# First mixer of a hybrid decoder step: the samples' split operand moved to its source, the states scaled on VectorE, a third of the weights' low parts built by adding loads

## The chip, the cores and the metric

The kernel runs on one core of a Trainium2 chip. The metric is the device time of one execution in microseconds. The engines are named as in the profile: PE (TensorE, matmuls; PEld is its weight load), DVE (VectorE), ACT (ScalarE), POOL (GpSimd), SP (SyncE, which only issues DMAs here).

## The reference, cut to what matters

The program is one inference step of a two-layer decoder on 512 prompt tokens and 8 sequences of 4 sample tokens (T = 544 columns). Each layer is a token mixer and a squared-ReLU MLP. Layer 0 has a Mamba-2 mixer, layer 1 an HGRN2 mixer. The change is in the Mamba-2 mixer:

```python
proj = u @ w_in                                   # 1024 x 5152: gates z, x, B, C, dt
xbc  = silu(conv4(x | B | C) + conv_b)
# chunked scan, for 32 heads in 4 groups
w = (C B^T) * exp(cum_i - cum_j) * dt             # inside a chunk
y = w @ x + (C h) * exp(cum)                      # from the state before it
h = exp(cum_last) * h + sum_j tail_j x_j B_j^T    # state after it
y = group_rmsnorm((y + D * x) * silu(z)) @ w_out
```

The states of the 8 sample sequences go through the same recurrence: `h = decay * h + outer(tail * x, B)`.

## The kernel before

**Products.** All columns sit in tiles of 128 x 544. A weight unit is a tile of 128 x 1024 (512 KB) that SP loads to `raw`. It is split in two parts that TensorE can multiply at one pass each: ACT casts `whi`, and `wlo = raw - whi` is taken by DVE, or, for the units 6, 9, ... 54 of the first mixer (`3 < u < U_MLP`, `u % 3 == 0`, 17 of its 56 units), by POOL. `products` then does hi x hi, hi x lo and lo x hi for each of 8 (or 2 x 4) row tiles and two column halves: 48 matmuls of 128 x 272 a unit.

**Order.** `ORDER` lists the mixer's units by hand: 4 gate units z, 6 input units i (four of x, then B and C) and 4 output units o for each of 4 groups. `conv_unit` splits the weights one to two units ahead of the product, and issues the loads from a list (`loads`), by a number ahead. Beside the products run generators: `scan(g)` (the recurrence of group g) and `gated_norm(g)`. `products` calls `tick()` after every 12 matmuls, which steps them; `yield pace` in them says after how many ticks the next piece follows. From that program a scheduler with priorities orders each engine's instructions; engines run their lists strictly in order, and semaphores carry the dependences.

**The scan of a group.** `tokens(c)` transposes x of chunk c (`pxt`) and scales it to `xd` (DVE) and `xt` (ACT, 8 small operations). `weights(c)` loads `w` (cumulated decays, 8 heads x 128 x 128) and makes relu and exp of it on ACT; `weighted(c)` multiplies by `cb` on DVE. `inside(c)` adds to the state `hT` (`pu`; its scaling by `dec` on POOL) and to the outputs (`py`). `before(c)` loads the decays a second time as `E`, takes exp, and adds the old state's part (`pi`).

For the samples `xts` is made from `pxs`, and later, two pieces on, `xq`, its hi and lo parts in 32-row bands (ACT cast, then two DVE subtractions of 32 x 512 on the other bands). `psi` reads the old states `st` (four tiles of two sequences). Then POOL scales all four `st` by the decays, and in four steps two matmuls `pn` (`bm` x `xq`, PSUM tiles from the pool `mx` of 4, which `pu`, `py`, `psi`, `pi` share) are added by DVE to `st`, which SP stores.

Of the kernel before, what the change touches and what calls it, by code (L numbers as in the profile page):

```python
# [16 lines left out]
P = 128  # L17
D = 1024
# [78 lines left out]
def trunk(ctx: ExitStack, tc: tile.TileContext, io):  # L97
# [65 lines left out]
    mp = {}  # L163

# [25 lines left out]
    def conv_unit():  # L190
        if state["conv"] >= len(jobs):
            return
        (kind, u), at = jobs[state["conv"]]
        state["conv"] += 1
        with tc.high_priority() if u > 2 else ExitStack():
            while state["load"] <= min(at + (3 if mp else 1), len(loads) - 1):
                if loads[state["load"]][0] != "u" and not mp:
                    break
                load_next()
        with tc.high_priority() if u > 2 and not mp else ExitStack():  # L200
            if kind == "u":
                raw = loaded.pop(("u", u))
                hi = wcv.tile([P, 1024], F32R, tag="whi", name=f"whi{u}")
                lo = wcv.tile([P, 1024], F32R, tag="wlo", name=f"wlo{u}")
                for a in (0, 512) if u < 2 else (None,):
                    c = slice(None) if a is None else slice(a, a + 512)
                    split(raw[:, c], hi[:, c], lo[:, c], nc.gpsimd if 3 < u < U_MLP and u % 3 == 0 else None)
            else:
                hi, lo = form(kind, u)
        ready[kind, u] = (hi, lo)  # L210

# [66 lines left out]
    def products(ps, hi, lo, ops, first, last):  # L278

        n = len(ops)  # L280
        for k, (oh, ol) in enumerate(ops):
            for j, (w, o) in enumerate(((hi, oh), (hi, ol), (lo, oh))):
                for h in range(2):
                    nc.tensor.matmul(  # L284
                        ps[:, h, :HF], w[:, k, :], o[:, h * HF : (h + 1) * HF],
                        start=(first and k == 0 and j == 0), stop=(last and k == n - 1 and j == 2),
                    )
            if k % 2:
                tick()
# [49 lines left out]
    def add_squares(t, first, name):  # L339
        if first:  # L340
            nc.scalar.activation(ssq[:, :T], t, AF.Square)
        else:
            sq = nt.tile([P, 568], F32, tag="t", name=name)[:, :T]
            nc.scalar.activation(sq, t, AF.Square)
            nc.vector.tensor_tensor(ssq[:, :T], ssq[:, :T], sq, ADD)
# [32 lines left out]
    def ssd(then):  # L378
# [5 lines left out]
        wdt = pool.tile([P, KT, NS], F32, tag="cm", name="wdt")  # L384
# [5 lines left out]
        seqcol = cp.tile([P, SEQS, NS], F32, name="seqcol")  # L390
        nc.sync.dma_start(seqcol, io["seqcol"])
# [37 lines left out]
        def conv_tile(u, ct, dst, rep):  # L429

            hi, lo = unit(u)
            ps = acc_tile(f"ps{u}")
            products(
                ps, hi.rearrange("p (k m) -> p k m", m=P), lo.rearrange("p (k m) -> p k m", m=P), uops, True, True
            )
            pre = p2.tile([P, 571], F32, tag="pre", name=f"pre{ct}")
            sv = pre[:, 515:571].rearrange("p (s t) -> p s t", t=7)
            nc.gpsimd.memset(pre[:, 0:3], 0.0)
            nc.scalar.copy(pre[:, 3:275], ps[:, 0, :HF])
            nc.scalar.copy(pre[:, 275:515], ps[:, 1, :240])  # L440
# [3 lines left out]
            acc = pool.tile([P, 568], F32, tag="cacc", name=f"cacc{ct}")  # L444
            wc = V_CONVW - V_CONVB + ct
            nc.scalar.activation(acc, pre[:, 0:568], AF.Identity, bias=vh[:, ct : ct + 1], scale=vh[:, wc : wc + 1])
            for i in range(1, 4):
                nc.vector.scalar_tensor_tensor(acc, pre[:, i : i + 568], vh[:, wc + 24 * i : wc + 24 * i + 1], acc, MUL, ADD)
            th = nt.tile([P, 568], F32, tag="t", name=f"th{ct}")
# [3 lines left out]
            for s0, n in ((0, 7), (7, 1)):  # L453
                a = [t[:, 515 + 7 * s0 : 515 + 7 * s0 + (7 * n if n > 1 else 4)] for t in (th, acc)]
                if n > 1:
                    a = [t.rearrange("p (s t) -> p s t", t=7)[:, :, 0:4] for t in a]
                    d = dst[:, NP_ : NP_ + 28].rearrange("p (s t) -> p s t", t=4)
                else:
                    d = dst[:, NP_ + 28 : T]
                nc.vector.scalar_tensor_tensor(d, a[0], 1.0, a[1], ADD, MUL)  # L460
# [18 lines left out]
        def silu2(u, zs, z):  # L479

            th = nt.tile([P, 568], F32, tag="t", name=f"thz{u}")[:, :T]
# [3 lines left out]
        def first_gates():  # L485
# [11 lines left out]
            background(rstd_steps(1.0 / D, "sn", res, cp, wait=2), "sn", wait=2)  # L497
# [15 lines left out]
        def normed():  # L513

            for k in range(KT):
                t = pool.tile([P, T], F32, tag="st", bufs=4, name=f"xn{k}")
                if k % 3 == 1:
                    nc.gpsimd.tensor_tensor(t, x[k], rb, MUL)
                    scaled_split(t, vec[:, V_NMIX0 + k : V_NMIX0 + k + 1], *new_uops(k, "s"))
                else:  # L520
                    nc.vector.scalar_tensor_tensor(t, x[k], vec[:, V_NMIX0 + k : V_NMIX0 + k + 1], rb, MUL, MUL)
                    split(t, *new_uops(k, "s"))
                yield 0.8
# [3 lines left out]
        def scan(g, BT, CT, xs, par):  # L527
# [5 lines left out]
            sts, ws_, xds, xts = [], [], [], []  # L533
            hT = pool.tile([P, 512], F32, tag="hT", name=f"hT{g}")

            def weights(c):

                w = pool.tile([P, 8, P], F32, tag="w", bufs=2, name=f"w{g}_{c}")
                nc.sync.dma_start(w, cum_d[hs, c * P : (c + 1) * P].partition_broadcast(P))
# [3 lines left out]
                ws_.append(w)  # L543

            def tokens(c):
# [9 lines left out]
                for h in range(8):  # L555
                    nc.scalar.activation(xt[:, h], pxt[:, h * 64 : (h + 1) * 64], AF.Copy, scale=ttok[:, c, 8 * g + h : 8 * g + h + 1])
# [3 lines left out]
            def inside(c):  # L560
# [18 lines left out]
            def before(c):  # L579

                cs = slice(c * P, (c + 1) * P)
                E = pool.tile([P, 4, P], F32, tag="E", bufs=2, name=f"E{g}_{c}")
                src = cum_d[hs, cs].rearrange("(j o) t -> o j t", o=2)
                for o in range(2):
                    nc.sync.dma_start(E[64 * o : 64 * o + 64], src[o].partition_broadcast(64))
                nc.scalar.activation(E, E, AF.Exp)
# [12 lines left out]

            tokens(0)  # L600
            weights(0)
            yield pace
# [14 lines left out]
            nc.scalar.copy(bt.rearrange("p a b -> p (a b)"), pbt)  # L617
            cb = pool.tile([P, 4, P], F32, tag="cb", name=f"cb{g}")
# [6 lines left out]
            inside(0)  # L625
            yield pace
# [4 lines left out]
            weights(2)  # L631
            yield pace
            inside(1)
            yield pace
# [4 lines left out]
            weights(3)  # L639
            yield pace  # L640
            inside(2)
            yield pace
# [3 lines left out]
            cm = pool.tile([P, SEQS, NS], F32, tag="cm", name=f"cm{g}")  # L646
            nc.vector.tensor_tensor(cm, CT[:, sc].unsqueeze(1).to_broadcast([P, SEQS, NS]), seqcol, MUL)
# [10 lines left out]
            )  # L658
            pbs = mx(f"pbs{g}")
# [7 lines left out]
            ws = pool.tile([NS, 8, NS], F32, tag="ws", name=f"ws{g}")  # L667
# [13 lines left out]
            xq = pool.tile([P, 8, 64], F32R, tag="xt", bufs=2, name=f"xq{g}")  # L681
            nc.scalar.copy(xq, xt)
            for r in (32, 96):
                rs = slice(r, r + 32)
                nc.vector.tensor_tensor(xq[rs], xt[rs], xq[rs].bitcast(F32), SUB)
            yield pace
            psi = mx(f"psi{g}")
            for s in range(SEQS):
                c = s % 4
                nc.tensor.matmul(  # L690
                    psi[32 * c : 32 * c + 32, :], cm[:, s], sts[s // 2][:, s % 2], start=(s < 4), stop=(s >= 4),
# [5 lines left out]
            )  # L697
            for q in range(4):
                nc.gpsimd.tensor_tensor(
# [3 lines left out]
            yield 2 * pace  # L703
            for q in range(4):
# [173 lines left out]
        for u, (kind, g, j) in enumerate(ORDER):  # L878
# [3 lines left out]
            else:  # L882
                {"i": input_unit, "z": gate_unit, "o": out_unit}[kind](u, g, j)
        es.close()
# [633 lines left out]
```

## Time and profile before

| | |
|---|---|
| runs | 1583.47, 1586.29, 1589.55 us (median 1586.29) |
| profiled execution | 1590.45 us, of which the span of instructions is 1588.7 us |
| PE busy | 1547.5 us, 97% |
| DVE / ACT / POOL busy | 1099.3 / 741.9 / 187.9 us |
| TensorE clock granted | 0.985 on average |

Times within the trace count from the span's start. The first mixer fills about the first 500 us; then follow MLP, second mixer, MLP. "Idle ... <-" names the work that ended last before an instruction could start. A window's row gives for each engine the busy time and, in brackets, the number of instructions; PEclk is the granted clock of TensorE as a share of the full one.

### The profile page before, as it was taken

The page shows a single profiled execution, that of the slowest core. Times are in us where ns is not written, and L with a number is a line of the kernel's source. Part 1 is how long each engine was busy: PE and PEld are TensorE (multiplying, and loading weights), DVE is VectorE, ACT ScalarE, POOL GpSimd, SP SyncE. Part 2 cuts the span into 40 slices and gives each one's busy share as a digit, 9 for nine tenths or more (in the row PEclk, how much of TensorE's full clock was granted, in tenths as well). Part 3 has the DMA queues.
Part 4 walks back from the last instruction along what each step waited for, and adds up shares of the span by engine and source line. Part 5 has one row for each costly group of instructions (what it writes and reads, how often), then busy time and mean ns, then how long its engine had stood idle before and what let it go on. Part 6 is the DMA issues. An engine that isn't in the chain of part 4 may idle for free.

```text
span 1588.7 us, 32391 instructions
## 1 busy us (share of the span) xinstructions
PE 1547.5 (97%) x13420; PEld 1482.7 (93%) x13420; DVE 1099.3 (69%) x1962; ACT 741.9 (47%) x1431; POOL 187.9 (12%) x208
## 2 busy tenths in 40 slices
PE   8898989999999999999999999999999999999997
PEld 7896879999999999999999999999999999999997
DVE  7888787877887747464565688888878655474644
ACT  5585663757434526353463333333335436273552
POOL 4323141232311001010000000000001001010001
PEclk9998998999999999999999999999999999999998
DMA  5353435354236236344323232323226335453311
GB/s 185 104 164 105 159 88 187 102 176 143 74 120 175 91 107 172 94 136 104 112 64 126 67 96 83 98 83 116 77 94 173 88 106 153 120 160 80 120 54 57
DMA packets 88116, 183.28 MB, mean 115 GB/s; under 512 B 12641, under 2 KB 39297, under 8 KB 87969
## 3 DMA queue, kind: packets, MB, share of 16 engines
q1 hardware_dynamic: 79792, 167.49, 33.7%
q0 software_dynamic: 6912, 12.59, 4.9%
q8 instruction: 105, 1.72, 0.5%
q10 hardware_dynamic: 1264, 1.14, 0.2%
q14 instruction: 43, 0.34, 0.1%
HBM read 164.00 MB, written 17.18 MB: 114 GB/s over the span
## 4 chain that ended last, share of the span: by engine, by line
PE 71%; DVE 4%; ACT 1%; DMA 1%; issue 1%; POOL 0%; POOLq 0%; SPq 0%; ACTq 0%; DVEq 0%
PE pd L284 22%; PE ps L284 15%; PE pp L973 11%; PE pm L284 6%; PE pc L973 4%; PE pho L284 3%; PE po L284 2%; PE pa L1112 1%; DVE wlo L188 1%; ACT whi L187 1%; DMA raw<-in_W 1%; PE pS L1215 0%; PE po L1238 0%; PE pa L1131 0%; PE pd L1342 0%
## 5 line engine op out<-in xcount | busy, mean ns | idle before, releaser
L187 ACT CAST whi<-raw 128x1024 fp32r<-128x1024 f32 (+1 forms) x178 | 185.0, 1039 | 344.7 <-PE ps L284 110.7
L188 DVE TENSOR_TENSOR wlo<-raw,whi 128x1024 fp32r<-128x1024 f32 (+1 forms) x161 | 200.5, 1245 | 31.0 <-ACT whi L187 27.0
L284 PE MATMUL pd<-gh,wlo 128*128 128x272 f32 x992 | 205.5, 288 | 0.9 <-DVE wlo L188 0.6
L284 PE MATMUL pd<-gh,whi 128*128 128x272 f32 x992 | 205.7, 287 | 0.0
L284 PE MATMUL pd<-gl,whi 128*128 128x272 f32 x992 | 205.0, 288 | 0.0
L284 PEld LDWEIGHTS pd<-gh,wlo 128*128 128x128 f32 x992 | 155.7, 188 | 2.2 <-DVE wlo L188 2.2
L284 PEld LDWEIGHTS pd<-gh,whi 128*128 128x128 f32 x992 | 156.2, 188 | 0.0
L284 PEld LDWEIGHTS pd<-gl,whi 128*128 128x128 f32 x992 | 155.6, 188 | 0.0
L284 PE MATMUL ps<-uh_s,whi 128*128 128x272 f32 x576 | 127.4, 303 | 1.6 <-DVE zs L503 0.8
L373 DVE TENSOR_TENSOR x<-pd,x 128x544 f32<-128x544 f32 x62 | 44.7, 722 | 121.3 <-PE pd L284 121.3
L284 PE MATMUL ps<-ul_s,whi 128*128 128x272 f32 x576 | 122.5, 294 | 0.5 <-DVE ul_s L188 0.5
L284 PE MATMUL ps<-uh_s,wlo 128*128 128x272 f32 x576 | 121.7, 293 | 0.0
L180 POOL DMA_DIRECT2D v<-in_W x48 | 42.3, 1045 | 593.0 <-DMA v<-in_W 448.6
L284 PE MATMUL ps<-uh,whi 128*128 128x272 f32 x512 | 112.2, 300 | 0.0
L284 PE MATMUL ps<-uh,wlo 128*128 128x272 f32 x512 | 106.8, 288 | 0.0
L284 PE MATMUL ps<-ul,whi 128*128 128x272 f32 x512 | 106.4, 289 | 0.0
L284 PEld LDWEIGHTS ps<-uh_s,whi 128*128 128x128 f32 x576 | 93.0, 194 | 9.7 <-issue 5.6
L284 PEld LDWEIGHTS ps<-ul_s,whi 128*128 128x128 f32 x576 | 93.6, 195 | 1.0 <-DVE ul_s L188 0.7
L284 PEld LDWEIGHTS ps<-uh_s,wlo 128*128 128x128 f32 x576 | 92.7, 193 | 0.1
L284 PEld LDWEIGHTS ps<-uh,whi 128*128 128x128 f32 x512 | 80.6, 189 | 3.8 <-issue 1.4
L284 PEld LDWEIGHTS ps<-ul,whi 128*128 128x128 f32 x512 | 80.3, 189 | 0.0
L284 PEld LDWEIGHTS ps<-uh,wlo 128*128 128x128 f32 x512 | 80.2, 188 | 0.0
(428 smaller groups left out, 3894.1 us busy)
## 6 DMA issues: line engine op xcount, KB each, us to landing
raw<-in_W SPq DMA_DIRECT2D x198, 512.0 KB, 3.6
v<-in_W SPq DMA_DIRECT2D x48, 256.0 KB, 4.3
v<-in_W POOLq DMA_DIRECT2D x48, 256.0 KB, 5.8
st<-in_ssm_in SPq DMA_DIRECT2D x16, 512.0 KB, 5.7
w<-cum_d SPq DMA_DIRECT2D x16, 512.0 KB, 5.2
out_ssm_s<-st SPq DMA_DIRECT2D x16, 512.0 KB, 3.7
a<-in_W SPq DMA_DIRECT2D x24, 256.0 KB, 4.0
hst<-in_hgrn_in SPq DMA_DIRECT2D x8, 512.0 KB, 3.7
```

The costliest lines, as they stand in the source:

```text
L180: nc.gpsimd.dma_start(raw[:, c : c + 512], io["W"][u + 1][:, :512], accum_op=ADD)
L187: nc.scalar.copy(hi, raw)
L188: (eng or nc.vector).tensor_tensor(lo, raw, hi.bitcast(F32), SUB)
L284: nc.tensor.matmul(ps[:, h, :HF], w[:, k, :], o[:, h * HF : (h + 1) * HF], start=(first and k == 0 and j == 0), stop=(last and k == n - 1 ...
L373: nc.vector.tensor_tensor(v3(x[m]), ps[:, :, :HF], v3(x[m]), ADD)
L973: nc.tensor.matmul(ps, w[:, k, :], o, start=(name_ in ("p1", "p2", "q7") and k == 0 and j == 0), stop=(k == 3 and j == 2), skip_group_chec ...
L1112: nc.tensor.matmul(pv4[b * NS : (b + 1) * NS, c], K[:, bs], QQ[:, 2 - n :, bs], start=True, stop=True, tile_position=(0, b * NS),)
```

## The change

All of it lies in the first mixer.

1. **Sample operand.** `xq` is made right after `xts`, at high priority, in the slot of `cb` instead of one of `xt`.
2. **Scaling.** `st` is scaled by DVE, tile by tile just ahead of the two additions to it. So is `hT`, and `xt` is made by one DVE multiplication in place of 8 ACT operations. The normed columns of the start (`xn`) are all made on DVE (three were POOL's).
3. **Low parts.** For the 17 units, ACT writes `-whi`: with a scale of -1 in the float32r type, thus the negated high part. Two DMAs issued by POOL then add the same weights from HBM to it (`accum_op=ADD`), which leaves raw - whi. There is one such tile (`wlo`, `bufs=1`). It is asked for when the unit before is split. Loads go two units ahead instead of one.
4. **Order in `products`.** In this mixer the low parts come last in every four row tiles.
5. **Smaller.** `E` is taken by ACT from the loaded `w` (two operations of 64 x 512 in place of a load and one of 128 x 512). The rows `w` are loaded ahead of their use. The copy `bt` of the transposed B is at high priority. `cm` keeps its zeros and is filled by a copy. Two small operations of the convolution's tail become one.

```diff
-            while state["load"] <= min(at + (3 if mp else 1), len(loads) - 1):
+            while state["load"] <= min(at + (3 if mp else 2 if "w" in sp else 1), len(loads) - 1):
...
+                if added(u):
+                    nc.scalar.copy(hi, raw)
+                    lo = lows.pop(u)
...
+                if added(u + 1):
+                    added_low(u + 1)
...
+        lows[u] = sp["w"].tile([P, 1024], F32R, tag="wlo", bufs=1, name=f"wlo{u}")
+        nc.scalar.activation(lows[u], raw, AF.Copy, scale=-1.0)
+        for c in (0, 512):
+            nc.gpsimd.dma_start(lows[u][:, c : c + 512], io["W"][u][:, c : c + 512], accum_op=ADD)
...
+            order = [(k, j) for k0 in range(0, n, 4) for js in ((0, 1), (2,)) for k in range(k0, min(k0 + 4, n)) for j in js]
...
+                        nc.scalar.activation(E[os_], w[os_].rearrange("p (j o) t -> p o j t", o=2)[:, o], AF.Exp)
...
-                    nc.sync.dma_start(E[64 * o : 64 * o + 64], src[o].partition_broadcast(64))
-                nc.scalar.activation(E, E, AF.Exp)
...
-                for h in range(8):
-                    nc.scalar.activation(xt[:, h], pxt[:, h * 64 : (h + 1) * 64], AF.Copy, scale=ttok[:, c, 8 * g + h : 8 * g + h + 1])
+                nc.vector.tensor_tensor(
+                    xt, pxt.rearrange("p (h q) -> p h q", q=64), ttok[:, c, hs].unsqueeze(2).to_broadcast([P, 8, 64]), MUL
+                )
...
-                    nc.gpsimd.tensor_tensor(hv, hv, dec[:, hs, c : c + 1].to_broadcast([P, 8, 64]), MUL)
+                    nc.vector.tensor_tensor(hv, hv, dec[:, hs, c : c + 1].to_broadcast([P, 8, 64]), MUL)
...
+            with tc.high_priority():
+                nc.scalar.copy(bt.rearrange("p a b -> p (a b)"), pbt)
...
+            xq = pool.tile([P, 512], F32R, tag="cb", name=f"xq{g}").rearrange("p (h q) -> p h q", q=64)
+            with tc.high_priority():
+                nc.scalar.copy(xq, xt)
...
+            yield 2 * pace
             for q in range(4):
-                nc.gpsimd.tensor_tensor(
+                nc.vector.tensor_tensor(
                     sts[q].rearrange("p s (h q) -> p s h q", q=64), sts[q].rearrange("p s (h q) -> p s h q", q=64),
                     dec[:, hs, 4 + 2 * q : 6 + 2 * q].rearrange("p h s -> p s h").unsqueeze(3).to_broadcast([P, 2, 8, 64]), MUL,
                 )
-            yield 2 * pace
-            for q in range(4):
                 for i in range(2):
```

What the scheduler makes of it, at three places.

**The states of group 1, on DVE, before.** `xq` (the operand of `pn`) is split after `y` of chunk 3; the scaling of `st` is not on this engine.

```order
L448 SCALAR_TENSOR_TENSOR cacc_2542<-pre_2535,vh,cacc_2542 128x568
L591 TENSOR_TENSOR y_2152<-y_2152,E_3_2572 128x4x128
L570 TENSOR_TENSOR hT_2088<-pu_3_2604,hT_2088 128x512
L451 SCALAR_TENSOR_TENSOR xs_2_2400<-th_2547,cacc_2542 128x512
L460 SCALAR_TENSOR_TENSOR xs_2_2400<-th_2547,cacc_2542 128x28
L460 SCALAR_TENSOR_TENSOR xs_2_2400<-th_2547,cacc_2542 128x4
L577 TENSOR_TENSOR y_2152<-py_3_2608,y_2152 128x4x128
L685 TENSOR_TENSOR xq_2619<-xts_2519,xq_2619 32x512 x2
L373 TENSOR_TENSOR x<-po_0_1_2624,x 128x544
L695 TENSOR_TENSOR ysc_2646<-psi_2637,etok 128x512
L188 TENSOR_TENSOR wlo_2676<-raw_2553,whi_2675 128x1024
L709 TENSOR_TENSOR st_0_2089<-pn_0_2664,st_0_2089 128x512
```

And now, from the same place on:

```order
L606 TENSOR_TENSOR y_2112<-py_3_2549,y_2112 128x4x128
L398 TENSOR_TENSOR x<-po_0_1_2561,x 128x544
L189 TENSOR_TENSOR wlo_2610<-raw_2352,whi_2609 128x1024
L480 SCALAR_TENSOR_TENSOR xs_2_2351<-th_2495,cacc_2490 128x512
L483 SCALAR_TENSOR_TENSOR xs_2_2351<-th_2495,cacc_2490 128x32
L599 TENSOR_TENSOR hT_2060<-pu_3_2545,hT_2060 128x512
L727 TENSOR_TENSOR ysc_2583<-psi_2574,etok 128x512
L732 TENSOR_TENSOR st_0_2061<-st_0_2061,dec 128x1024
L732 TENSOR_TENSOR st_1_2063<-st_1_2063,dec 128x1024
L740 TENSOR_TENSOR st_0_2061<-pn_0_2598,st_0_2061 128x512
L189 TENSOR_TENSOR wlo_2721<-raw_2500,whi_2720 128x1024
```

`xq` has gone ahead (it stands nine rows above the first one shown), two scalings of `st` now stand ahead of the first addition, and the addition to `hT` (which frees the PSUM slot that the second `pn` takes) stands behind a split of weights.

**The start of group 1's scan, on PE, before.** `ps21` is the product of unit 21; `pbt` and `pcb` are the transposes of B and the product of B and C; `pu` reads `bt`, ACT's copy of `pbt`.

```order
L612 MATMUL pbt1_2216<-ident_77,BC1_4_1534 128x128 x4
L615 MATMUL pcb1_2217<-BC1_5_1688,BC1_4_1534 128x128 x4
L564 MATMUL pu1_0_2292<-xt1_0_2104,bt1_2226 128x512
L284 MATMUL ps21_2267<-uh0_s_413,whi21_2163 128x272 x2
L284 MATMUL ps21_2267<-ul0_s_414,whi21_2163 128x272 x2
L284 MATMUL ps21_2267<-uh0_s_413,wlo21_2164 128x272 x2
```

And now, two rows behind `pcb` (four matmuls left out):

```order
L309 MATMUL ps21_2225<-uh1_s_433,whi21_2123 128x272 x2
L309 MATMUL ps21_2225<-ul1_s_434,whi21_2123 128x272 x2
L309 MATMUL ps21_2225<-uh2_s_451,whi21_2123 128x272 x2
L309 MATMUL ps21_2225<-ul2_s_452,whi21_2123 128x272 x2
L309 MATMUL ps21_2225<-uh3_s_469,whi21_2123 128x272 x2
L309 MATMUL ps21_2225<-ul3_s_470,whi21_2123 128x272 x2
L309 MATMUL ps21_2225<-uh0_s_415,wlo21_1992 128x272 x2
L309 MATMUL ps21_2225<-uh1_s_433,wlo21_1992 128x272 x2
L309 MATMUL ps21_2225<-uh2_s_451,wlo21_1992 128x272 x2
L309 MATMUL ps21_2225<-uh3_s_469,wlo21_1992 128x272 x2
L593 MATMUL pu1_0_2250<-xt1_0_2078,bt1_2184 128x512
```

24 products of the next unit now stand between the transposes and the first reader of their copy. The last eight read an added low part (`wlo21`).

**The low parts, on POOL, before** (a stretch of group 1):

```order
L569 TENSOR_TENSOR hT_2088<-hT_2088,dec 128x512 x2
L438 MEMSET pre_2764 128x3
L442 COPY pre_2764<-cst 128x8x3
L188 TENSOR_TENSOR wlo_2556<-raw_2401,whi_2555 128x1024
L462 COPY xs_1_2260<-xs_1_2260 128x96
L569 TENSOR_TENSOR hT_2088<-hT_2088,dec 128x512
```

Now on POOL:

```order
L465 MEMSET pre_2870 128x3
L469 COPY pre_2870<-cst 128x8x3
L485 COPY xs_2_2351<-xs_2_2351 128x96
L230 DMA wlo_2724<-in_W 128x512 x2
L465 MEMSET pre_3032 128x3
```

and on ACT, which must have written the negated high part first:

```order
L568 ACTIVATE E_2_2322<-w_2_2263 64x512
L188 CAST whi_2354<-raw_2121 128x1024
L228 ACTIVATE wlo_2358<-raw_2219 128x1024
L568 ACTIVATE E_2_2322<-w_2_2263 64x512
L570 ACTIVATE w_2_2263<-w_2_2263,tok 128x128 x8
```

POOL keeps only memsets, copies of the convolution's edges and the issue of DMAs in this mixer. The negated part follows the cast of the unit before, and the DMA's issue waits behind copies that wait for DVE (`xs`).

More of the change, by code (lines that the diff above doesn't have):

```diff
@@ L625, in scan @@
             inside(0)
+            rows(2)
             yield pace
@@ L630, in scan @@
             before(1)
-            weights(2)
             yield pace
             inside(1)
+            rows(3)
+            weights(2)
             yield pace
@@ L680, in scan @@
             nc.sync.dma_start(io["ssm_p"][g], hT)
[L681 to L685, printed above, removed]
             yield pace
```

110 lines of the change are left out of this document (62 added, 48 removed).

## The prediction

> **What bounds the kernel now.** I read the page first, then the windows around the slices in which PE is not full, then PE's waits, then the order of time at the longest of them.
>
> ```profile
> PE 1547.5 (97%) x13420; PEld 1482.7 (93%) x13420; DVE 1099.3 (69%) x1962; ACT 741.9 (47%) x1431; POOL 187.9 (12%) x208
> ```
>
> PE is the bound. A busy PE is not one at full clock, though, so the loss has to be taken as width of a window minus busy time x granted clock:
>
> ```profile
> core 0: us, PE busy (x) PEld busy (x) DVE busy (x) ACT busy (x) POOL busy (x), PEclk, DMA share, GB/s
> 40.00:50.00 10.00, 8.62 (x64) 8.21 (x65) 8.95 (x12) 3.82 (x7) 4.90 (x3) 1.00 0.16 52
> 60.00:80.00 20.00, 17.58 (x114) 15.65 (x113) 15.69 (x31) 10.72 (x24) 5.37 (x7) 0.83 0.52 154
> 130.00:160.00 30.00, 22.14 (x160) 19.03 (x159) 27.96 (x41) 14.61 (x33) 12.01 (x13) 0.83 0.43 138
> 190.00:200.00 10.00, 6.78 (x29) 5.56 (x28) 6.98 (x8) 6.68 (x14) 0.25 (x2) 0.66 0.28 85
> 230.00:250.00 20.00, 14.26 (x96) 13.35 (x96) 15.52 (x21) 6.72 (x14) 6.84 (x4) 0.83 0.40 145
> 250.00:270.00 20.00, 18.12 (x122) 17.90 (x121) 14.90 (x30) 7.69 (x14) 3.99 (x4) 0.83 0.64 207
> 510.00:560.00 50.00, 50.00 (x400) 50.00 (x400) 38.20 (x62) 24.09 (x35) 0.00 (x0) 1.00 0.31 95
> ```
>
> The last row is what full work looks like: 8 matmuls a us, 0.125 us each. Losses by place: F (40 to 50) 1.4; E (60 to 80) 20 - 17.58 x 0.83 = 5.4; A (130 to 160) 30 - 22.14 x 0.83 = 11.6; B (190 to 200) 10 - 6.78 x 0.66 = 5.5; C (230 to 250) 8.2; D (250 to 270) 5.0. Together 37.1 us, all in the first mixer. In E, C and D the clock of 0.83 over 20 us means a stretch of 6.8 us at half clock, which costs up to 3.4 us beside the wait itself. The waits:
>
> ```profile
> PE pn L708 <- DVE xq L685: 13.6, 2, 7.9
> PE pu L564 <- ACT bt L617: 3.2, 1, 3.2
> PE gn_pc L319 <- DVE ssq L345: 2.0, 2, 1.9
> PE pdec L819 <- DVE dt_md L809: 1.6, 1, 1.6
> PE ps L284 <- DVE zs L503: 0.8, 1, 0.8
> ```
>
> The two of `xq` lie in A and C, `bt` is B, `ssq` D, `dt_md` E, `zs` F. In order of time at A:
>
> ```profile
> 134.34 0.67 DVE L570 TENSOR_TENSOR hT<-pu,hT 128x512 f32<-128x512 f32 x1
> 134.51 9.61 POOL L699 TENSOR_TENSOR st<-st,dec 128x1024 f32<-128x1024 f32 x4
> 134.94 2.11 DVE L448 SCALAR_TENSOR_TENSOR cacc<-pre,vh,cacc 128x568 f32<-128x568 f32 x1
> 137.57 2.36 DVE L188 TENSOR_TENSOR wlo<-raw,whi 128x1024 fp32r<-128x1024 f32 x1
> 139.85 2.47 DVE L448 SCALAR_TENSOR_TENSOR cacc<-pre,vh,cacc 128x568 f32<-128x568 f32 x1
> 142.35 2.30 DVE L685 TENSOR_TENSOR xq<-xts,xq 32x512 fp32r<-32x512 f32 x1
> 145.53 0.69 DVE L685 TENSOR_TENSOR xq<-xts,xq 32x512 fp32r<-32x512 f32 x1
> 146.36 1.19 PE L708 MATMUL pn<-xq,bm 128*128 128x512 f32 x2 [7.86 <-DVE xq L685]
> ```
>
> While POOL scales the states, each DVE operation on SBUF takes 2.1 to 2.5 us. The second half of `xq`, behind POOL's work, takes 0.69. So it is POOL's elementwise work that makes DVE late, and `xq` is at the end of that queue.
>
> **The change part by part.** Prices, all from the first 500 us:
>
> ```profile
> L188 POOL TENSOR_TENSOR wlo<-raw,whi 128x1024 fp32r<-128x1024 f32 x17 | 42.2, 2485 | 115.3 <-ACT whi L187 115.3
> L699 POOL TENSOR_TENSOR st<-st,dec 128x1024 f32<-128x1024 f32 x16 | 34.9, 2208 | 5.0 <-PE psi L690 5.0
> L598 DVE TENSOR_TENSOR w<-w,cb 128x1024 f32<-128x1024 f32 x16 | 19.4, 1221 | 6.0 <-ACT w L542 5.9
> L709 DVE TENSOR_TENSOR st<-pn,st 128x512 f32<-128x512 f32 x32 | 20.9, 681 | 5.8 <-PE pn L708 3.2 <-POOL st L699 1.3 <-issue 1.2
> L187 ACT CAST whi<-raw 128x1024 fp32r<-128x1024 f32 x53 | 55.6, 1049 | 57.7 <-PE ps L284 23.6 <-issue 21.0 <-PE po L284 7.9
> L586 ACT ACTIVATE E<-E 128x512 f32<-128x512 f32 x12 | 7.7, 639 | 7.4 <-DMA E<-cum_d 7.4
> ```
>
> *Load of DVE.* It gains 16 scalings of `st` at 1.22 us (the row of `w`, the same 128 x 1024), 12 of `hT` and 16 of `xt` at 0.68, and three operations of the `xn`, about 0.7 each: 40.7 us. It gets back what POOL's operations cost it. In the 9.6 us of A the first four stretched operations took 9.24 us; by the unstretched rows (1.22 for 1024 columns, 0.68 for 512, and 0.75 put for 568 between them, an estimate) they are 3.4. So 5.8 us are lost in 9.6 us of POOL, 0.6 for each us. 42.2 and 34.9 us of POOL then make 46 us. The bounds are 0 and 77. DVE's load is about even, and its work no longer comes in stretched pieces. ACT loses 128 small operations for `xt`, gains 17 negations at 1.05 and 12 half tiles of `E` at up to 0.64, which the same 128 operations cover. The loads of `E` (two for each of 12) vanish from SP. The `w` loads stand earlier on it, and raw loads go one more unit ahead; what this does to SP's queue I bound at 0 to 2 us and take as 0, since a load has a unit (6 us, 48 matmuls) more of time.
>
> *A, group 0's states.* Once `xq` is early, PE and DVE run a race behind `pxs` (the transposes that begin the samples' part), and the PSUM slot that the second `pn` takes is freed by the addition to `hT`. PE's pieces from the chain in order of time, later in the same mixer:
>
> ```profile
> 386.13 0.89 PE pi L589 x8
> 388.54 0.86 PE pu L564 x2
> 389.39 1.02 PE py L573 x16
> 406.96 1.85 PE psi L690 x16
> ```
>
> By the order, PE has from `pxs` to the second `pn` 60 matmuls (7.5 us), `pi`, `pu`, `py`, `psi` (4.6), and small ones with the first `pn` (0.7): 12.8 us. DVE has up to that addition seven operations of 512 columns and the two of `xq` (0.60 each, the spacing from the row at 134.34 to its follower at 134.94), five of 568 (0.73, in that ratio), one of 1024 (1.15) and small ones (0.8): 11.0 us. So DVE is 1.8 us ahead, if it starts on time. Before it did not:
>
> ```profile
> 124.48 0.60 PE L650 MATMUL pxs<-ident,xs 128*128 128x128 f32 x4
> 127.90 0.68 DVE L652 TENSOR_TENSOR xds<-pxs,tok 128x512 f32<-128x512 f32 x1
> ```
>
> `xds` began 2.8 us after the end of `pxs`, behind an operation stretched by POOL's split. I leave it as late, since ACT's weights of chunk 3, which DVE multiplies ahead of it, now queue behind a negation: a wait of 1.0 us stays. So does what is lost in `psi`, some 1.7 us (1.85 for eight, of 32 columns of the array each, is mostly not work at full rate; an estimate). A falls from 11.6 to 2.7: gain 8.9 (bounds 4 and 10).
>
> *C, group 1's states.* The same sum: PE 48 matmuls of products up to the first `pn`, then five, 6.6 us in all, with 4.6, and 0.7, is 12.0 us. On DVE the first addition to `x` waits for `po_0_0` (4.2 us after `pxs`). From there stand 0.6 for it, 1.2 for `xq`, ten of 512 to 568 columns (6.6), 1.15 for the split of weights and 0.7 of small ones: 14.4. PE waits 2.4 us where it waited 5.7. Whether the clock falls for it is open: D's wait of 1.9 us brought a half-clock stretch, and F's of 0.8 us brought none. I count half of its 3.4 us. C keeps 2.4 + 1.7: gain 4.1 (bounds 0 and 8). [...]
>
> *B, the copy `bt`.*
>
> ```profile
> 186.03 3.39 ACT L556 ACTIVATE xt<-pxt,ttok 128x64 f32<-128x64 f32 x16 [0.25 <-DVE xd L551]
> 193.20 0.69 ACT L617 COPY bt<-pbt 128x512 f32<-128x512 f32 x1
> 193.95 2.08 PE L564 MATMUL pu<-xt,bt 128*128 128x512 f32 x2 [3.22 <-ACT bt L617]
> ```
>
> ACT loses the 3.39 us of `xt` ahead of it, and PE has 24 matmuls (3.0 us) in between. Either covers the 3.2. Gain 5.0 of 5.5 (bounds 0 and 5.5); if the cover is gone, `pu` waits as before.
>
> *D, E, F.* `ssq`, `dt_md` and `xn` were stretched by POOL's split or product beside them. `gn_pc` also stands 27 instead of 38 matmuls into its unit, but 128 instead of 86 behind `pys`. Gains 4.0 of 5.0, 3.5 of 5.4 (small matmuls stay), 0.8 of 1.4; bounds 0 to 5, 0 to 5, -1 to 1.4.
>
> *The added low parts.*
>
> ```profile
> v<-in_W POOLq DMA_DIRECT2D x48, 256.0 KB, 5.8
> L180 POOL DMA_DIRECT2D v<-in_W x19: 856/865/1222, 499.6 to 768.1; - x19
> DMA to landing us min/median/max: 3.4/4.3/10.6
> ```
>
> The MLPs already use such loads: 5.8 us to landing, and no load of `v` in the window of the second row took over 10.6. From the release of the tile (the low part of three units before, or the cast ahead of it) a unit needs the cast 1.05, the negation 1.05, two issues 1.7 and the landing 5.8: 9.6 us. By the order the tightest of the 17 has two units and 16 matmuls of products, 14 us. Even a landing of 10.6 (14.4) is only 0.4 late, and the low parts' place at the end of four row tiles is in the 14. Queued behind the negation on ACT are `pre` copies and `w`; behind the issue on POOL, copies for the convolution. Both have a unit's time. I take -2 us for the whole (two late ones of 1 us), with bounds 0 and -17 (all by 1 us), and for DVE elsewhere -1.5 (0 to -6: its rows are close to PE's time in groups 0 and 1).
>
> *Sum.* 8.9 + 5.0 + 4.1 + 4.0 + 3.5 + 0.8 - 2 - 1.5 = 22.8 us. Against the profiled execution's 1590.45 that is 1567.7. The median of the runs, 1586.3, is 4.2 lower, and with it the forecast is 1563.5. Nothing behind the first mixer changes.
>
> **The rivals.**
>
> - *DVE becomes the bound in groups 0 and 1.* For it: DVE is busy 27.96 of 30 us in A, and my sums there are even. Against it: part of that is stretch. Then A and C gain 3 in place of 13.0, and the others hold: gain 12.8, 1573.5.
> - *All the waits go and no new one comes.* The 37.1 us without what stays (1.7 in A, 0.5 in B): about 35, so 1551. Against it is C's sum.
> - *The added parts come late: slower.* Place: the low products of every third unit. It decides once the chain needs 14 us and, of the gain without loads, 24.8/17 = 1.5 us more on average, that is a landing near 11.7 us. All 17 at 2.5 us late cost 42.5: 1586.3 - 24.8 + 42.5 = 1604, without the clock. For it: the loads read-modify-write what other traffic fills at 0.35 to 0.64 share in these rows. Against: the median of 5.8.
> - *POOL's issue is held up by DVE's work.* An issue is 0.86 to 1.22 us in the rows; if each waited for one DVE operation of 1.22 us more, the chain is 12.0 us and still early: no change of the sum. Only at twice that, 5 us a pair, is it 14.6 and each unit 0.6 late, 10 us or 8 more than counted: 1571.5. [...] The rows of the MLP, with DVE 76% busy (38.20 of 50), don't show it.
> - *Nothing moves:* POOL's stretch goes, but DVE's new work takes its place everywhere: 1586.
>
> **How the numbers follow.** Chances: forecast 0.55, DVE as the bound or a held issue 0.18, all waits gone 0.12, late parts 0.09, nothing 0.06. A measurement can tell 0.5% (7.9 us, from 1586.3 to 1578.4) from no change. Faster: 0.55 + 0.15 + 0.12, less a little for unnamed ones: 0.80; same: 0.11; slower: 0.09. The range leaves out the last two cases: it goes from 1547 (all waits gone, and 4 us of what I let stay) to 1580 (DVE as the bound, with half of B, D, E and F besides).
>
> **What would show it.** Right: no wait of `pn` on `xq` and no wait of `pu` on `bt` over 1 us; PE's clock without half stretches but perhaps one at C; POOL under 40 us in the first mixer; `cacc` at its unstretched time everywhere; the low products of units 6, 9, ... without a wait on a DMA. Wrong: `pn` waiting on `hT` or `st` for more than 3 us in groups 0 and 1 (first rival), or PE waiting on `wlo` from a load (third).

## The result, and the profile after

| | us | runs |
|---|---|---|
| before | 1587.5 (1583.5 to 1589.6) | 5 |
| after | 1574.4 (1573.0 to 1577.7) | 5 |
| ratio | 0.9924, 95% interval 0.9905 to 0.9942 | |
| predicted | 1563.5, range 1547 to 1580 | |

The change gains 13 us where 22.8 were forecast. In the profiled executions it is 1590.45 to 1573.53, 16.9 us, since the profiled execution of before lay 3 us above its median and that of after 0.9 below; the places below are read in these two. The whole core first, then the windows of the prediction (and the stretches between them), then PE's longest waits behind 40 us, all of the kernel after:

```profile
PE 1539.2 (98%) x13420; PEld 1477.0 (94%) x13420; DVE 1081.3 (69%) x1985; ACT 741.6 (47%) x1332; POOL 122.4 (8%) x195
```

```profile
core 0: us, PE busy (x) PEld busy (x) DVE busy (x) ACT busy (x) POOL busy (x), PEclk, DMA share, GB/s
40.00:50.00 10.00, 9.10 (x72) 9.13 (x73) 8.80 (x15) 5.13 (x8) 1.33 (x1) 1.00 0.17 52
60.00:80.00 20.00, 20.00 (x156) 19.14 (x155) 15.72 (x29) 13.79 (x30) 3.35 (x11) 1.00 0.84 241
100.00:130.00 30.00, 26.71 (x213) 23.48 (x213) 20.22 (x32) 16.87 (x39) 2.26 (x5) 0.96 0.44 110
130.00:160.00 30.00, 28.30 (x207) 24.91 (x204) 28.02 (x42) 16.46 (x33) 9.52 (x13) 0.93 0.64 181
160.00:190.00 30.00, 25.05 (x177) 24.91 (x177) 19.29 (x42) 19.54 (x34) 1.75 (x2) 0.83 0.50 146
190.00:200.00 10.00, 10.00 (x86) 9.07 (x85) 9.54 (x14) 3.12 (x7) 0.52 (x3) 1.00 0.44 108
230.00:250.00 20.00, 20.00 (x163) 19.45 (x163) 17.86 (x27) 8.09 (x15) 4.90 (x5) 1.00 0.84 262
250.00:270.00 20.00, 20.00 (x165) 20.00 (x164) 17.03 (x35) 14.42 (x28) 3.08 (x8) 1.00 0.67 187
```

```profile
PE ps L309 <- DVE zs L506: 6.7, 1, 6.7
PE py L602 <- DVE xts L687: 3.3, 1, 3.3
PE ps L309 <- DVE zs L526: 1.5, 1, 1.5
PE po L309 <- DVE yl L189: 1.1, 1, 1.1
PE py L602 <- DVE w L623: 0.9, 2, 0.6
PE po L309 <- ACT yh L188: 0.7, 1, 0.7
PE pn L739 <- DVE y L606: 0.7, 1, 0.7
```

Places E (60 to 80), B (190 to 200), C and D (230 to 270) are full and at full clock. The waits on `xq`, `bt`, `ssq` and `dt_md` are gone. Two long new waits have come, 3.3 us at `py` and 6.7 us ahead of a unit of products, both in group 0; each has a half-clock stretch (granted clock 0.50), of 6.8 and 10.2 us, which pulls down the clock in 100 to 190. (The two waits of `po` lie near 450 us, ahead of the last output units; they are new too, and brought no half-clock stretch: the clock is 1.00 in 440 to 480.)

That DVE's work is no longer stretched shows best at the convolution's operations, all of one size; first before, then after:

```profile
L448 DVE SCALAR_TENSOR_TENSOR cacc<-pre,vh,cacc x72: 787/804/2473, 54.1 to 373.0; 128x568 f32<-128x568 f32 x72
L476 DVE SCALAR_TENSOR_TENSOR cacc<-pre,vh,cacc x72: 787/802/812, 52.1 to 354.8; 128x568 f32<-128x568 f32 x72
```

The three numbers are the shortest, the median and the longest in ns.

Windows of equal times hold different work in the two kernels. So the second table goes by work: 48 product matmuls make a unit, and the gain at a unit is when its first matmul begins before, less when it begins after (us, worked out from the two traces).

| first matmul of unit | before | after | gain so far | what lies between |
|---|---|---|---|---|
| 9 | 81.73 | 75.40 | 6.33 | F and E |
| 14 | 122.98 | 117.63 | 5.35 | |
| 15 | 134.84 | 135.64 | -0.80 | new wait of `py`: -6.2 |
| 17 | 161.76 | 149.60 | 12.15 | A's waits on `xq` gone, `pys` moved behind unit 17's start: +13.0 |
| 19 | 175.19 | 175.50 | -0.32 | new wait ahead of unit 18, `pys` moved here: -12.5 |
| 24 | 229.63 | 224.42 | 5.22 | B: +5.5 |
| 32 | 303.19 | 285.24 | 17.95 | C and D: +12.7 |
| 56 | 867.42 | 849.30 | 18.12 | |

The matmuls of `pys` and one of `pn`, 2.4 us together, stood ahead of unit 17 before and stand behind its start now. Without them A gained 10.6 us and the new wait ahead of unit 18 cost 10.1: the wait of 6.65, and about half of the 7.05 us at half clock that were left when it ended.

**The wait of `py`, in order of time** (the first row is `py` of chunk 1, whose end at 107.9 frees the tile of `w` that chunk 3's rows need):

```profile
106.80 1.09 PE L602 MATMUL py<-w,xd 128*64 128x128 f32 x16
109.66 1.22 DVE L189 TENSOR_TENSOR wlo<-raw,whi 128x1024 fp32r<-128x1024 f32 x1 [2.81 <-ACT whi L188]
110.91 0.33 SPq L171 DMA_DIRECT2D raw<-in_W  x1
111.29 0.43 SPq L558 DMA_DIRECT2D w<-cum_d  x1
119.92 1.29 ACT L568 ACTIVATE E<-w 64x512 f32<-64x512 f32 x2 [6.02 <-DMA w<-cum_d]
124.81 1.23 DVE L623 TENSOR_TENSOR w<-w,cb 128x1024 f32<-128x1024 f32 x1 [3.10 <-ACT w L571]
127.45 0.67 DVE L687 TENSOR_TENSOR xts<-pxs,ttok 128x512 f32<-128x512 f32 x1
128.27 1.98 PE L602 MATMUL py<-w,xd 128*64 128x128 f32 x16 [3.29 <-DVE xts L687]
```

The rows of `w` could go at 107.9. They stand in SP's queue behind a load of raw weights (unit 17's, by the order), and that one needs the tile which DVE's split frees at 110.9. They are issued at 111.3 and land 8.6 us later, beside that load and two adding loads. ACT stands idle for 6.0 us with `E` at the head of its queue, DVE then for 3.1 us, and `py` needs the PSUM slot that `xts` frees. Since the change makes `E` from `w`, ACT's first work on a chunk waits for this one load.

**The wait ahead of unit 18:**

```profile
152.61 0.30 PE L745 MATMUL pys<-sel,ysc 128*128 128x32 f32 x2
155.22 1.27 DVE L740 TENSOR_TENSOR st<-pn,st 128x512 f32<-128x512 f32 x2
157.33 1.05 ACT L188 CAST whi<-raw 128x1024 fp32r<-128x1024 f32 x1 [6.96 <-PE ps L309]
158.42 1.23 DVE L189 TENSOR_TENSOR wlo<-raw,whi 128x1024 fp32r<-128x1024 f32 x1 [1.92 <-ACT whi L188]
160.91 2.63 DVE L763 TENSOR_TENSOR y<-y,zs 128x544 f32<-128x544 f32 x4
164.09 0.71 DVE L506 SCALAR_TENSOR_TENSOR zs<-thz,ps 128x544 f32<-128x544 f32 x1
164.95 0.79 PE L309 MATMUL ps<-uh_s,whi 128*128 128x272 f32 x2 [6.65 <-DVE zs L506]
```

Unit 18 needs the accumulator of unit 16, which `zs` of unit 16 frees; that `zs` needs the tile of group 0's first `zs`, which the gate (`y<-y,zs`) frees; and the gate needs `pys`. By the order `pys` stood at unit 16 + 28 matmuls before and stands at 17 + 22 now, because the additions to the states, with their scalings on DVE, come later. So 26 matmuls (3.3 us) are left for that chain instead of 68 (8.5 us). The conversion of unit 19, which cannot begin before PE ends unit 17, stands ahead of the gate on ACT and DVE besides.

### The profile page after: what moved, and what is told of

The parts are those of the page before. It is cut to its first block, busy times and chain, and to the rows that moved or that the text cites. A ratio compares the mean times of both kernels' runs of the same rounds, so it can differ in the third digit from the quotient of the medians.

```text
span 1571.7 us, 32262 instructions
## 1 busy us (share of the span) xinstructions
PE 1539.2 (98%) x13420; PEld 1477.0 (94%) x13420; DVE 1081.3 (69%) x1985; ACT 741.6 (47%) x1332; POOL 122.4 (8%) x195
## 4 chain that ended last, share of the span: by engine, by line
PE 90%; DVE 3%; ACT 3%; DMA 2%; issue 1%; POOL 0%; POOLq 0%; SPq 0%; ACTq 0%; DVEq 0%
PE ps L309 25%; PE pd L309 23%; PE pp L1005 11%; PE pm L309 6%; PE po L309 6%; PE pc L1005 5%; PE pho L309 3%; DMA w<-cum_d 1%; DVE wlo L189 1%; PE pa L1144 1%; ACT whi L188 1%; PE py L602 1%; ACT w L570 1%; PE pS L1247 1%; PE po L1270 1%
## 5 line engine op out<-in xcount | busy, mean ns | idle before, releaser
L188 ACT CAST whi<-raw 128x1024 fp32r<-128x1024 f32 (+1 forms) x161 | 167.1, 1038 | 337.6 <-PE ps L309 110.5
L189 DVE TENSOR_TENSOR wlo<-raw,whi 128x1024 fp32r<-128x1024 f32 (+1 forms) x161 | 195.6, 1215 | 35.3 <-ACT whi L188 30.1
L309 PE MATMUL ps<-uh_s,wlo 128*128 128x272 f32 x576 | 85.6, 291 | 0.0
L309 PEld LDWEIGHTS ps<-uh_s,wlo 128*128 128x128 f32 x576 | 78.2, 191 | 0.0
```

The source lines that it names most:

```text
L188: nc.scalar.copy(hi, raw)
L189: (eng or nc.vector).tensor_tensor(lo, raw, hi.bitcast(F32), SUB)
L309: nc.tensor.matmul(ps[:, h, :HF], w[:, k, :], o[:, h * HF : (h + 1) * HF], start=(first and i == 0), stop=(last and i == len(order) - 1),)
```

## The experiments

Nine kernels, each timed in four runs or more beside the kernel before (1586.9 to 1588.1 there). Times are medians.

**e1: the raw load of unit 17 out of SP's queue.**

```diff
-            nc.sync.dma_start(raw, io["W"][u])
+            (nc.gpsimd if u == 17 else nc.sync).dma_start(raw, io["W"][u])
```

> The changed kernel with one load moved: the raw weights of unit 17 are issued by POOL, so that in SP's queue the rows of w for group 0's chunk 3 no longer stand behind them. Theory (SP's queue): the slot of those rows is free at 107.9, but the load of unit 17 ahead of it waits for DVE's split of unit 14 until 110.9, so the rows are issued 3 us late, ACT waits 6.0 us for them, DVE 3.1 for ACT, and py of chunk 3 waits 3.3 with a half-clock stretch of 6.8 us behind it. Then: issue near 108.0, py's wait at most 0.6, no half-clock stretch there, unit 15 begins some 6 us earlier, and the time is 1567 to 1569 (1574.4 now), with the second long wait (6.7 us, PE on zs) as it was. Rival (DVE is late at that place whatever the rows do): py still waits 2.5 us or more, 1573 to 1575. Rival (the landing of 8.6 us beside the added low loads is the cause): the rows land near 116.6 and a wait of 0.3 to 0.6 stays, so the time falls as well, but the landing stays at 8 us or more.

1570.2 us, ratio 0.9883 (0.9864 to 0.9902), 1.2 above the theory's range. In e1 the rows of `w` were issued at 107.8 and landed in 4.1 us; in the kernel after and in e2 (below), behind the raw load, it took 8.6 and 10.0. The rows of the loads' view in e1, after, e2, and in e7 (below), which has the same raw load ahead but no adding loads:

```profile
w<-cum_d SPq DMA_DIRECT2D x1, 512.0 KB, 4.1
```

```profile
w<-cum_d SPq DMA_DIRECT2D x1, 512.0 KB, 8.6
```

```profile
w<-cum_d SPq DMA_DIRECT2D x1, 512.0 KB, 10.0
```

```profile
w<-cum_d SPq DMA_DIRECT2D x1, 512.0 KB, 5.5
```

`py` does not wait, and unit 15 begins 6.4 us earlier than after the change. SP's queue it was; 3.5 us of it by the late issue and 4.5 by the landing, which the late issue had put among the other traffic. Of these 4.5 us some 3 go with the adding loads (8.6 against 5.5 in e7; 5.0 in e6, which has none either) and 1.4 with the raw load. So the adding loads, though never late themselves, had a part in this wait. That DVE is late there anyway is refuted. The wait ahead of unit 18 stayed at 6.7 us; its half-clock stretch became 13.65 us, and with a wait of 1.1 us at `pn` that took back 2.9 us by unit 19.

**e2: group 0's scaling back on POOL.**

```diff
-                nc.vector.tensor_tensor(
+                (nc.gpsimd if g == 0 else nc.vector).tensor_tensor(
                     sts[q].rearrange("p s (h q) -> p s h q", q=64), ...
```

> The changed kernel with the scaling of group 0's states (4 operations of 128 x 1024) back on POOL; groups 1 to 3 stay on DVE. With it the matmuls of pys stand at unit 16 + 31 matmuls again (before the change 16 + 28, after it 17 + 22). Theory (place): the wait of 6.7 us ahead of unit 18 is the chain pys, gate, thz and zs of unit 16, which frees the accumulator that unit 18 needs; it has 26 matmuls (3.3 us) after the change and 65 (8.1 us) here. Then that wait is under 1 us, its half-clock stretch of 10.2 us is gone, and the time is 1561 to 1565, with py's wait of 3.3 us as it was. Rival (load): DVE has as much to do as with the scaling on it, since four operations of 1.21 us go and POOL's four of 2.2 us stretch DVE's by 0.6 us for each us, 5.3 us; then PE still waits 4 us or more ahead of unit 18 or for pn, and the time is 1572 or more.

1568.7 us, 0.9878 (0.9860 to 0.9896), above the range of the place theory, but with what it says of the wait. The two waits of PE in e2 that bear on it:

```profile
PE py L602 <- DVE xts L687: 4.2, 1, 4.2
PE pn L739 <- DVE st L740: 1.6, 1, 1.6
```

There is no wait ahead of unit 18 and no half-clock stretch there. The wait of `py`, which the edit does not touch, was 0.9 us longer, and POOL's scaling brought 1.6 us at `pn` and 3.4 us at half clock. The place of `pys` decides; the load theory, which wanted 4 us or more left, is refuted.

**e3: the spacing of group 0's steps, 1.1 to 0.9.**

```diff
-PACE = (1.1, 0.9, 1.4, 0.8)
+PACE = (0.9, 0.9, 1.4, 0.8)
```

> The changed kernel with one number changed, the spacing of group 0's scan steps from 1.1 to 0.9 row tiles of products. Scaling stays on DVE. By the order the rows of w for chunk 3 stand ahead of unit 17's load on SP, and pys at unit 16 + 42 instead of 17 + 22. Theory (place and queue): both new waits of the changed kernel go or fall under 1.5 us each (54 matmuls, 6.8 us, for the chain behind pys), 1556 to 1562. Rival (load): DVE, busy 28.0 of 30 us at group 0's states, is the bound; the same work in fewer matmuls makes PE wait elsewhere (py, pn or unit 18), in total 8 us or more, 1570 to 1580.

1579.6 us, 0.9948 (0.9934 to 0.9962): both waits are gone, and a third is 8.0 us. PE's wait and, from the order of time, ACT and DVE ahead of it:

```profile
PE gn_pc L344 <- DVE ssq L370: 8.2, 2, 8.0
```

```profile
153.75 1.28 ACT L568 ACTIVATE E<-w 64x512 f32<-64x512 f32 x2 [5.86 <-DMA w<-cum_d]
157.46 0.73 DVE L370 TENSOR_TENSOR ssq<-ssq,gsq 128x544 f32<-128x544 f32 x1 [4.08 <-ACT gsq L369]
```

The time fits the load theory's figure, but not its reason: DVE stood idle 4.1 us, because ACT waited 5.9 us for rows of `w` again, now group 1's, with the gate's squares queued behind. These rows were issued at 143.4, behind a raw load, a store and two adding loads, and landed 10.3 us later: the landing's half of the first mechanism, at a second place. Nor is that wait all of the loss. At unit 19 e3 is 2.3 us behind the kernel after, at unit 32 it is 7.0: in group 1 PE waits 1.9 us for `pre` and 1.9 us for `st`, with a half-clock stretch of 6.83 us.

**e4: before, with `xq` made early and nothing else changed.**

```diff
+            xq = pool.tile([P, 512], F32R, tag="cb", name=f"xq{g}")...
+            with tc.high_priority():
+                nc.scalar.copy(xq, xt)          # and the two subtractions, ahead of pbs
...
-            xq = pool.tile([P, 8, 64], F32R, tag="xt", bufs=2, name=f"xq{g}")
-            nc.scalar.copy(xq, xt)              # behind inside(3)
```

> The kernel before with one part of the change alone: xq (the samples' split operand) is made right behind its source, ahead of pi and py of chunk 3; its tile is that of cb. Scaling, low parts and the rest stay on POOL. Theory (place of xq): the waits of pn on xq (7.9 and 5.7 us) fall under 1.5 us each by the move alone, with the half-clock stretches behind them; the waits on bt, ssq and dt_md stay: 1570 to 1576 (1587.5 before). Rival (POOL's stretch): DVE is late there by POOL's scaling, and with xq early PE waits as long for st, for the additions that free the slots of pn, or ahead of unit 18: 1583 or more.

1585.1 us, 0.9985 (0.9973 to 0.9996). PE no longer waits on `xq`, but at the same matmuls on what frees their PSUM slots; and DVE is stretched as it was:

```profile
PE pn L709 <- DVE y L577: 4.5, 2, 2.4
PE pn L709 <- DVE ysc L696: 2.7, 2, 1.9
```

```profile
138.68 2.59 DVE L188 TENSOR_TENSOR wlo<-raw,whi 128x1024 fp32r<-128x1024 f32 x1
```

So the early place of `xq` is worth 2 us alone: POOL's stretch was the cause and `xq` only the last in the queue, as the prediction read it. What its old place would cost without POOL's work no run shows. One thing more: the wait on `bt` is gone here too, although `xt` still takes 3.39 us of ACT, so for B the loss of `xt` on ACT is not what is needed.

**e5: both edits, of e1 and e2.**

> The changed kernel with both edits that each took one wait away: unit 17's load issued by POOL, and the scaling of group 0's states back on POOL. Theory (the two waits are separate): py of chunk 3 does not wait, nothing over 1 us ahead of unit 18, a wait of pn of some 1.6 us stays; gain at unit 19 some 12 us over the changed kernel: 1561 to 1565 (1574.4 changed, 1570.2 and 1568.7 with one edit each). Rival (the waits trade: PE, 6 us earlier, meets DVE late at the next place): PE waits 4 us or more for pn, st or ahead of unit 18, and the time is 1567 to 1570.

1561.6 us, 0.9839 (0.9826 to 0.9853): faster than both kernels, and 12.8 us below the kernel after. At unit 19 the gain over it is 10.9. PE's longest waits there behind 40 us, and the windows of group 0:

```profile
PE ps L309 <- DVE zs L526: 1.7, 1, 1.7
PE pn L739 <- DVE st L740: 1.6, 1, 1.6
```

```profile
100.00:130.00 30.00, 30.00 (x246) 25.29 (x246) 25.85 (x42) 21.77 (x51) 4.70 (x9) 1.00 0.51 127
130.00:160.00 30.00, 27.47 (x198) 25.57 (x197) 27.26 (x40) 14.29 (x26) 17.13 (x15) 0.94 0.68 213
```

The two waits are separate; taking one away does not feed the other.

**e6: the low parts back on POOL, all else as changed.**

```diff
-                if added(u):
-                    nc.scalar.copy(hi, raw)
-                    lo = lows.pop(u)
-                else: ...                       # and added_low(u + 1)
+                    split(raw[:, c], hi[:, c], lo[:, c], nc.gpsimd if added(u) else None)
```

> The changed kernel with the low parts of units 6, 9, ... 54 computed on POOL again, as before the change, in place of the negation and the adding loads; all else as changed. Theory (stretch): each of the 17 splits (2.5 us) stretches DVE beside it by 0.6 us for each us, 25 us in all, and at the places where DVE is waited for PE waits again: ssq, dt_md and the states, 6 to 10 us slower than the changed kernel, 1580 to 1585. Rival (the loads bring nothing by themselves, the gains are all of xq, xt and the scaling): within 2 us of 1574.4. Rival (their traffic costs more than POOL's splits: without them the rows of w land in 5 us in place of 8.6): 1568 to 1572, with py's wait of chunk 3 gone.

1592.4 us, 1.0026 (1.0013 to 1.0039), slower than before the change and 18 us slower than after it: the stretch theory, with twice its price. The rows of `w` landed in 5.0 us, as the last rival said, but that gain is small beside the loss. Waits came back at `pcb`, `pys`, `pn` and `gn_pc`; 2.0 us were left at `py`, and the wait ahead of unit 18 stayed:

```profile
PE ps L303 <- DVE zs L500: 6.6, 1, 6.6
PE pcb L636 <- DVE BC L474: 3.7, 2, 2.0
PE gn_pc L338 <- DVE ssq L364: 1.6, 1, 1.6
```

DVE's time above its unstretched durations (each operation against the 15th percentile of its kind, first 505 us) is 52.3 us before, 7.8 after and 29.2 here, 22.0 of it beside the 42.9 us of POOL's splits: 0.51 for each us.

The 18 us are not the price of these splits in the kernel before. Against the kernel after, e6 is 6.9 us behind at unit 19 and 10.6 at unit 48; 9.4 more are lost by unit 51, with two half-clock stretches of 6.83 us behind waits of 0.7 and 1.6 us, where the kernel before had none.

**e7: the low parts on DVE, no loads.** The same diff with `None` for POOL.

> The changed kernel with the 17 low parts on DVE (1.22 us each, 20.7 us more in the first mixer) and no negation, no adding load. Theory (DVE has no room in groups 0 and 1: it decides when PE goes on): PE waits there for 3 us or more beyond the two waits that the changed kernel has, 1577 to 1584. Rival (DVE has room, and the loads cost by their traffic and their negations on ACT): the rows of w land in 5 us, the wait of py goes, 1567 to 1573.

1576.8 us (1573.9 to 1577.9), 2.4 above the kernel after, with runs that overlap: neither theory. Without the adding loads and the negations the new wait of `py` falls to 0.4 us, as the rival had it, and the one ahead of unit 18 rises:

```profile
PE ps L303 <- DVE zs L500: 8.6, 1, 8.6
PE pn L733 <- DVE hT L593: 2.1, 2, 1.7
```

The order moved too: `pys` stands at unit 17 + 37 matmuls here, which leaves 11 matmuls for the chain behind it in place of 26, so the 8.6 us are not DVE's load alone. By the traces e7 is 3.7 us ahead of the kernel after at unit 15, has lost all of it by unit 18, and is 4.2 us behind at unit 56. So 20.7 us more of DVE cost few us, net of the gain at `py`: DVE has room, except where PE waits for its end.

By their edits e6 and e7 differ only in the engine of the 17 splits (the order moved with it), and e6 is 15.6 us slower: most of its loss comes not from the work itself, but from POOL doing it beside DVE.

**e8: both edits, and no scaling of states on DVE at all.**

> The kernel with both edits, and the scaling of the states on POOL in groups 1 to 3 too, so that no scaling of the states is left on DVE. Theory (stretch): in group 1, where the scaling on DVE went with a gain of 8 us or more, POOL's scaling brings waits of pn or ahead of a unit back: 3 us or more slower than the kernel with both edits. Rival (xq's early place and the low parts off POOL took those waits away, and the engine of the scaling is worth nothing in groups 1 to 3): within 2 us of it.

1568.9 us, 7.3 above e5, by one wait in group 1 with a half-clock stretch of 6.8 us that begins in it:

```profile
PE pn L739 <- DVE y L606: 5.3, 1, 5.3
```

The scaling on DVE is worth 7.3 us in groups 1 to 3 and costs 8.7 in group 0 (e5 against e1). The same edit has both signs, by what stands behind it.

**e9: e1, and unit 19's conversion on POOL** (cast and low part, `split` with POOL for `u == 19`).

> The changed kernel with unit 17's load issued by POOL and, beside it, the conversion of unit 19 (cast and low part) on POOL, so that on ACT and DVE it no longer stands ahead of group 0's gate and of zs of unit 16; the scaling of the states stays on DVE and pys stands at unit 17 + 22 as in the changed kernel. The wait ahead of unit 18 was 6.7 us: ACT's cast of unit 19 waits 7.0 us for the end of unit 17, DVE 1.9 us for it, and DVE then works 6.4 us, 1.2 of it the low part of unit 19. Theory (queue: the conversion ahead is all of it): the wait falls under 1 us, 1559 to 1563 (1570.2 with the load's move alone). Theory (place: the chain from pys to zs takes some 5 us of DVE and has 26 matmuls, 3.3 us): 3 to 4 us of the wait stay, with a half-clock stretch of 6.8 us, 1564 to 1568.

1568.6 us (1567.2 to 1570.0), 1.7 below e1 with runs that overlap, and above the range of either theory; the wait is still 6.2 us. DVE no longer waits 1.9 us for the cast nor works 1.2 at the low part, but POOL's copy and split beside the gate stretch the gate's four products from 2.63 to 5.29:

```profile
152.83 5.29 DVE L766 TENSOR_TENSOR y<-y,zs 128x544 f32<-128x544 f32 x4
154.08 2.82 POOL L192 TENSOR_TENSOR wlo<-raw,whi 128x1024 fp32r<-128x1024 f32 x1
```

Without that stretch it would be some 3.5 us (6.2 less 2.7, an estimate), which would be the place theory's 3 to 4. What of the 6.7 us was the conversion ahead is at most 3.1 (1.9 and 1.2); the edit brought its own disturbance, so the split of the two stays open.

## Why the prediction was right and where it failed

- **The cause: right.** POOL's elementwise work made DVE late. e4 shows it from the side of the kernel before, e6 beside e7 from that of the kernel after. DVE lost 44.5 us of stretch (52.3 to 7.8); the prediction put 46. Of its signs, no wait of `pn` on `xq` or of `pu` on `bt`, and `cacc` at its unstretched time, came true; a clock without half stretches but perhaps one at C did not: there are two, both in group 0.
- **The time lies in the range partly by luck.** The places forecast to gain gave 8.8 us more than the sum had, and the 2 us put aside for late low parts were not needed; against this stand 6.2 and 8.6 us that the sum did not have, of the two new waits, and 1.0 us between units 9 and 14.
- **F and E: 4.3 forecast, 6.3 measured. B: 5.0 and 5.5. C and D: 8.1 and 12.7.** C did not keep the wait of 2.4 us with half of a clock stretch: `pn` waited 0.7 us there and the clock held. The sum also left 1.7 us in C for what `psi` loses. But a loss was taken as width less busy time, and the profile counts `psi`'s matmuls as busy: those 1.7 us had never been in the 8.2. Which of DVE's terms made the forecast wait of 2.4 us too long was not tried.
- **A, the old wait: 8.9 forecast, 10.6 measured** (13.0 by the table, less the 2.4 us that moved): the stall and all of its half-clock stretch. Here too 1.7 us had been left in `psi` that were not in the loss.
- **The added low parts: -2 forecast for late ones, none was late.** No matmul waited on an adding load. The longest landing of the 34 in the first mixer, by the view of the tile, makes the chain 14.1 us (3.8 and 10.3), beside the 14 us of the tightest unit:

```profile
DMA to landing us min/median/max: 5.0/6.6/10.3
```

What they did cost is the 3 us that their traffic put on the landing of the rows of `w` in group 0 (e7 against the kernel after), which no term of the sum had.

- **The failed step is what was set to nothing on SP's queue.** The prediction wrote that `w` loads stand earlier and raw loads one unit further ahead, bounded that at 0 to 2 us and took 0, since a load has a unit more of time. The raw load has; the rows of `w` queued behind it had not. It measured 6.2 us by the table, and e1 got 6.4 back. At the same place a wait of 1.0 us was left in A, put down to the negation on ACT; it was 3.3 us with a stretch at half clock, and by the rows.
- **The second failed term is "DVE elsewhere", -1.5 with bounds 0 and -6: it measured -10.1**, all of it the wait ahead of unit 18 with its half clock. The prediction counted, for D, how far `gn_pc` stands behind `pys`. It did not do so for group 0's `pys`, which had moved 42 matmuls nearer to the unit that needs the accumulator. The order said so before any run. e2 put `pys` back and the wait was gone; how much of it the conversion of unit 19 adds stays open (e9).
- **The rivals.** "DVE becomes the bound" gives 1573.5, within 1 us of the result, by another way: it wanted A and C to gain only 3, while C gained in full and DVE stood idle for 3.1 and 1.9 us in the two new chains. The adding loads were not late, and their issue was not held up: the 34 issues took 0.85 to 1.22 us each, and a pair took 1.74 us (110.89 in the order of time), as counted; no run shows the 5 us more that the rival put on a pair. POOL under 40 us did not hold by the page's count (71 us up to 500), but that takes 40 issues of loads as busy, 35 us; the other work came to 36.
- **The clock.** Every half-clock stretch between 40 and 505 us in the eleven traces of this study lasts a multiple of 3.41 us (3.41, 6.83, 10.24 or 13.65). The length of a wait does not decide alone what stretch it brings: in e5 a wait of 1.6 us brought one of 3.41, while `gn_pc` waited 1.9 us before and in e4, with a stretch of 6.83 us before and none in e4. C's half price was a guess about a wait that did not come.

## What to carry to other kernels

When a load is moved ahead in a queue, price what stands behind it until its own tile is free, not the load: here the rows of `w` went at 111.3 in place of 107.8. When operations move to the engine that frees an accumulator, count by the order the matmuls from the last input of that chain to the matmul that needs the slot, in every group: here 68 became 26. And a gain that comes from ending contention should be tested by parts: one part alone was worth 2 us (e4), the whole without another part was a loss (e6), and two small undoings doubled the gain (e5).

## What the runs showed of the hardware that was not expected

- The same load of 512 KB landed in 4.1 us when issued ahead of a raw load and two adding loads, in 5.0 and 5.5 behind the raw load alone (e6, e7), and in 8.6 and 10.0 among all of them.
- The same wait of 6.7 us, with a half-clock stretch that begins in it, left 7.05 us at half clock behind it in the kernel after and 9.65 in e1 (stretches of 10.24 and 13.65), so the clock's part of a wait's price varied by 1.3 us between two runs with the same order at that place.
- DVE lost 0.51 us for each us of POOL's splits beside it in e6 (22.0 in 42.9). In e9 the gate's four operations took 5.29 us in place of 2.63 beside POOL's copy and split. In A the addition of `py`, which reads PSUM, took 0.68 us beside POOL's scalings, and the four other DVE operations there took 2.1 to 2.5 each. These four and the four scalings beside them took 10.1 us; one after the other they would take 11.3, an estimate from 1.94 us for a scaling with DVE idle beside it (e4) and the unstretched DVE times.
